# One pool for the normed blocks and the up weights, three early loads of the down part, and a written order for the last tiles of a hybrid decoder layer

## The chip, the cores and the metric

One NeuronCore of a Trainium2 chip runs the whole kernel. The metric is device time in microseconds of one execution. Five engines work side by side, each through its own queue in the order of that queue: TensorE (PE, matmuls; PEld are its weight loads), VectorE (DVE), ScalarE (ACT), GpSimd (POOL) and SyncE (SP), which here issues every DMA.

## The reference

One layer of a hybrid decoder in float32 on 1024 tokens of width 1024. Two mixers (gated DeltaNet and GLA) make `merged`; the change touches what follows. Cut to that:

```python
x = x + rms_norm(merged @ w_o[l], norm_mix_post[l])
h = rms_norm(x, norm_mlp_pre[l])
u = jnp.square(jax.nn.relu(h @ w_mlp_up[l]))          # 1024 -> 4096
x = x + rms_norm(u @ w_mlp_down[l], norm_mlp_post[l]) # 4096 -> 1024
```

## The kernel before

A float32 product is made of three matmuls: every operand is split into a high part (ACT, `CAST`, tiles `wh`, `s[:,0]`) and a low part (DVE, one subtraction, `wl`, `s[:,1]`), and `mm3` (L256) issues high x high, high x low, low x high. So each operand passes ACT and then DVE before PE can use it.

Both products of the channel mixer use a seven-product scheme on 2x2 blocks (Strassen's, in a form with few sums). The stages that matter here, in the order of the program:

1. **Out projection and norms** (L1060 to L1127, pool `op`). `merged @ w_o`, the two norms, and the transposes give four blocks of the normed input, `X11`, `X21`, `X12`, `X22`, 8 KB a partition each, and from them the seven split right-hand operands of the up product: `R11`, `R21`, `R22` in pool `hp2`, `T1` to `T4` in pool `bot` (tag `big`, four buffers).
2. **Early products** (L1129 to L1151). For the first NE = 8 units, products P1 and P2 (which need only `R11` and `R21`) are made ahead, in pairs of units; their results `e` are stored to `d_p` and `d_u[0]` in DRAM and loaded again later by `again` (tiles `p1`, `c11`). Behind them stand the splits of `T3` and `T4` (L1152 to L1156).
3. **Up** (L1194 to L1354, pool `ml`). 16 units n. `prep(n)` (L1200) loads the unit's up weights as two DMAs into one tile `wu` (three buffers) and makes four sums on DVE (`ss`, and one in place). Then the products P6, P5, P7, P3, P4 (for n >= 8 also P1 and P2), 12 matmuls each, accumulate in two PSUM banks: `A` (names `mr`, `mo`) and `C` (name `g`). Between two products that share a bank, a result is read out (`from_A`, L1246; the sums with `C`), and the next product into that bank waits for it. `u_sums` (L1313) makes three more sums and stores seven blocks to DRAM (`d_u`). For n >= 8 `down_sums` (L1226) also loads blocks of the down weights and stores two sums of them to DRAM (`d_t`); it and `u_sums` share the tag `us` with seven buffers.
4. **Down** (L1357 to L1440, pool `dn`). Seven products P1, P2, P6, P5, P7, P4, P3 of eight steps; a step is 24 matmuls on a pair of row blocks. `fetch` (L1175) loads `ru` from `d_u` and `rv` from the down weights or `d_t` (512 KB each, two buffers), and for two products `rx`, and splits them into `s4` (three buffers). One step, the first of P1, is fetched ahead within the last unit of up (L1347 to L1349), into the places of `R11` and `R21`. The scale of the last norm's weight (L1408) is on ACT.
5. **Last tiles** (L1437 to L1440). As each of the four last banks of P3 is done: a sum (DVE), a square with its row sum (ACT, `jk`), a product with the norm weight (DVE), the inverse root (two POOL operations on `sums`), two `scalar_tensor_tensor` on DVE, two stores. The scheduler orders these.

The order in each engine's queue is made by a list scheduler when the kernel is built: by the order of the program, with priorities (`tc.high_priority`), and by when a buffer of a tag comes free. A pool that is opened where a closed one lay takes its bytes, and a tile in it waits for the old tiles that it covers. Before, pool `ml` lies where `op` lay. Each DMA in SP's queue waits in its turn for the tiles it needs, and all behind it wait too.

Of the kernel before, what the change touches and what calls it, by code (L numbers as in the profile page):

```python
# [16 lines left out]
P = 128  # L17
# [115 lines left out]
def kernel(  # L133
# [923 lines left out]
    wdn = wview(w_mlp_down[0], 32)  # L1057


    with tc.tile_pool(name="op", bufs=1, reuse_waits="tile") as op:  # L1060
        X = {n: op.tile([P, 4, 512], F32, name="X" + n) for n in ("11", "21", "12", "22")}
# [9 lines left out]
        for u in range(2):  # L1071
# [19 lines left out]
            for i in range(4):  # L1091
# [6 lines left out]
                xt = op.tile([P, D], F32, tag="xt", name="xt", bufs=2)  # L1098
# [30 lines left out]
        for n in range(0, NE, 2):  # L1129
            pair = range(n, n + 2)  # L1130
            bank = {}
            for p, k0, blk in (("P1", 0, R["11"]), ("P2", 4, R["21"])):
                for m in pair:
# [17 lines left out]
                    SP.dma_start(out=d_p[m] if p == "P1" else d_u[0][:, m, :], in_=e)  # L1151
        T3, T4 = big(), big()  # L1152
# [17 lines left out]
    def load(pool, tag, src):  # L1170
        raw = pool.tile([P, 2, 512], F32, tag=tag, name=tag, bufs=2) if tag else pool
        SP.dma_start(out=raw, in_=src)
        return raw

    def fetch(p, j, pool, place=None):  # L1175
        b, src, *more = LR[p]
        if place:
            s4, (u, v) = place
# [15 lines left out]
    NU = 16  # L1194
    with tc.tile_pool(name="ml", bufs=1, reuse_waits="tile") as ml:
        RT = dict(P1=R["11"], P2=R["21"], P3=R["22"], P4=T4, P5=T1, P6=T2, P7=T3)
        un = {}
        reserve(ml, (("ev", 512, 10), ("us", 512, 7), ("wu", 2 * KT * P, 3)))

        def prep(n):  # L1200
            raw = ml.tile([P, 2 * KT * P], F32, tag="wu", name="wu", bufs=3).rearrange("p (f k c) -> p f k c", f=2, c=P)
            for f in range(2):
                c0 = (n + NU * f) * P
                SP.dma_start(out=raw[:, f], in_=wup[:, :, c0:c0 + P])
# [150 lines left out]
    bot.release()  # L1355


    with tc.tile_pool(name="dn", bufs=1, reuse_waits="tile") as dn:
        def keep(nm):
            return [dn.tile([P, 512], F32, name=f"{nm}{i}") for i in range(4)]  # L1360

        c12, c22 = keep("c12"), keep("c22")
        reserve(dn, (("xt", D, 4),))
# [43 lines left out]
        c11, c21 = keep("c11"), keep("c21")  # L1407
        act(wpost2, wpost2, AF.Copy, scale=D ** 0.5)  # L1408
# [28 lines left out]
        for i in products("P3", Bb, False, True):  # L1437
            tt(c12[i], Bb[i], c12[i], ALU.add)
# [33 lines left out]
```

## Time and profile before

| | us |
|---|---|
| median of 3 runs | 1728.85 |
| range of the runs | 1727.12 to 1730.13 |
| the profiled execution, its own time | 1728.73 |
| the profiled execution, span of the page | 1727.0 |
| PE busy | 1657.5 (96%) |
| DVE busy | 986.5 (57%) |
| ACT busy | 771.7 (45%) |
| POOL busy | 131.6 (8%) |

The span runs from the first to the last instruction; 1.73 us of the time lie around it. A row of the timeline has start, duration, engine, line, operation, the tiles written and read, and in square brackets how long the engine stood idle before it and what released it. SPq rows are DMA issues. A row of a windows table gives busy time and count of each engine in that stretch, the granted clock of PE, the share of the DMA engines' time, and GB/s.

### The profile page before, as it was taken

The numbers are of one execution on the slowest core, as the hardware profiler recorded it, in microseconds if no ns is written. First come the engines' busy times: TensorE is split into PE (matmuls) and PEld (weight loads), VectorE is DVE, ScalarE is ACT, GpSimd is POOL, SyncE is SP. The second block draws the span as 40 slices with busy tenths as digits, with TensorE's granted clock in tenths as the row PEclk, the third lists the DMA queues.
The fourth block names the chain that finished last, engine by engine and source line by source line (L and its number), as shares of the span: only waits on it lengthen the run. The fifth ranks groups of instructions, "written<-read, shape, count | busy, mean of one in ns | idle before, by whom it ended". The sixth has DMA issues, their size and how long they took to land.

```text
span 1727.0 us, 24474 instructions
## 1 busy us (share of the span) xinstructions
PE 1657.5 (96%) x9174; PEld 1401.2 (81%) x9174; DVE 986.5 (57%) x1678; ACT 771.7 (45%) x1577; POOL 131.6 (8%) x221
## 2 busy tenths in 40 slices
PE   7999999999999999999999999889999979999997
PEld 6887778878899998998788877667788858888886
DVE  5677565862544436642445365777777754555664
ACT  5456545643533335433321255634455544443442
POOL 2010111111001000101000021000000000000021
PEclk9999999999999999999999999989999989999999
DMA  5222213322211121124634344566588888577775
GB/s 165 56 77 70 83 41 89 86 68 70 67 49 50 50 62 44 37 62 158 204 108 140 129 161 155 176 227 218 184 276 293 270 273 279 192 237 246 231 253 184
DMA packets 186405, 251.39 MB, mean 146 GB/s; under 512 B 23351, under 2 KB 108430, under 8 KB 186286
## 3 DMA queue, kind: packets, MB, share of 16 engines
q1 hardware_dynamic: 186286, 249.83, 45.0%
q8 instruction: 72, 1.18, 0.3%
q14 instruction: 47, 0.39, 0.1%
HBM read 185.79 MB, written 63.98 MB: 145 GB/s over the span
## 4 chain that ended last, share of the span: by engine, by line
PE 81%; DVE 6%; ACT 5%; DMA 5%; issue 2%; POOL 1%; SPq 0%; DVEq 0%; ACTq 0%; POOLq 0%
PE g L67 55%; PE mr L67 9%; PE mo L67 8%; PE ml L67 3%; PE mt L67 3%; DMA gb<-d_g 2%; PE mt L71 1%; DVE Xt L165 1%; DVE Xi L547 1%; ACT wh L236 1%; ACT E L177 1%; DMA oraw<-d_ob 1%; DVE wl L165 1%; DMA d_sig<-sg 1%; ACT Zp L603 0%
## 5 line engine op out<-in xcount | busy, mean ns | idle before, releaser
L165 DVE TENSOR_TENSOR wl<-w,wh 128x512 fp32r<-128x512 f32 x181 | 125.7, 695 | 229.6 <-ACT wh L236 228.1
L67 PE MATMUL g<-hT,wh 128*128 128x512 f32 (+1 forms) x600 | 239.5, 399 | 1.3 <-DVE gr L174 0.9
L67 PE MATMUL g<-hL,wh 128*128 128x512 f32 (+1 forms) x600 | 233.1, 388 | 0.0
L67 PE MATMUL g<-hT,wl 128*128 128x512 f32 (+1 forms) x600 | 232.3, 388 | 0.0
L236 ACT CAST wh<-w 128x512 fp32r<-128x512 f32 x184 | 114.0, 619 | 212.6 <-PE g L67 189.1
L67 PE MATMUL g<-s 128*128 128x512 f32 x768 | 177.6, 393 | 11.6 <-ACT s L1189 11.6
L67 PE MATMUL g<-wh,hT 128*128 128x256 f32 x640 | 185.1, 289 | 0.0
L67 PE MATMUL g<-wl,hT 128*128 128x256 f32 x640 | 181.5, 284 | 0.0
L67 PE MATMUL g<-wh,hL 128*128 128x256 f32 x640 | 181.4, 284 | 0.0
L67 PEld LDWEIGHTS g<-s 128*128 128x128 f32 x768 | 145.6, 190 | 43.0 <-ACT s L1189 12.0
L165 DVE TENSOR_TENSOR s<-ru,s 128x1024 fp32r<-128x1024 f32 x55 | 67.4, 1225 | 124.6 <-ACT s L1189 124.3
L67 PEld LDWEIGHTS g<-hT,wh 128*128 128x128 f32 x600 | 113.8, 190 | 21.6 <-DVE gr L174 1.1
L67 PEld LDWEIGHTS g<-hT,wl 128*128 128x128 f32 x600 | 113.7, 189 | 21.6 <-DVE wl L165 0.2
L67 PEld LDWEIGHTS g<-hL,wh 128*128 128x128 f32 x600 | 113.9, 190 | 18.7 <-issue 1.0
L1189 ACT CAST s<-ru 128x1024 fp32r<-128x1024 f32 x55 | 57.9, 1053 | 150.9 <-PE g L67 73.0
L67 PEld LDWEIGHTS g<-wh,hT 128*128 128x128 f32 x640 | 122.4, 191 | 1.4 <-issue 1.0
L67 PEld LDWEIGHTS g<-wl,hT 128*128 128x128 f32 x640 | 122.6, 191 | 1.2 <-issue 1.0
L67 PEld LDWEIGHTS g<-wh,hL 128*128 128x128 f32 x640 | 122.5, 191 | 0.1
L177 ACT ACTIVATE c<-c 128x512 f32<-128x512 f32 x104 | 64.8, 631 | 38.8 <-DVE c L165 37.2
L67 PE MATMUL g<-wh,big 128*128 128x512 f32 x256 | 80.4, 392 | 0.0
L67 PE MATMUL mr<-big,wh 128*128 128x512 f32 x192 | 61.7, 403 | 11.1 <-ACT wh L236 11.1
L165 DVE TENSOR_TENSOR s<-rv,s 128x1024 fp32r<-128x1024 f32 x55 | 67.0, 1219 | 3.2 <-ACT s L1189 3.2
(419 smaller groups left out, 3383.7 us busy)
## 6 DMA issues: line engine op xcount, KB each, us to landing
ru<-d_u SPq DMA_DIRECT2D x55, 512.0 KB, 4.3
w<-in_w_in_dram SPq DMA_DIRECT2D x80, 256.0 KB, 2.7
rv<-in_w_mlp_down_dram SPq DMA_DIRECT2D x39, 512.0 KB, 5.4
wu<-in_w_mlp_up_dram SPq DMA_DIRECT2D x32, 512.0 KB, 5.1
d_u<-c SPq DMA_DIRECT2D x56, 256.0 KB, 2.8
d_u<-us SPq DMA_DIRECT2D x48, 256.0 KB, 2.0
us<-in_w_mlp_down_dram SPq DMA_DIRECT2D x48, 256.0 KB, 4.7
xt<-in_x_dram SPq DMA_DIRECT2D x16, 512.0 KB, 5.2
```

Of the source, the lines that this page charges most:

```text
L67: return self.eng.matmul(out, lhsT, rhs, start=start, stop=stop, skip_group_check=more)
L71: return self.eng.transpose(out=out, in_=in_, identity=identity)
L165: (eng or V).tensor_tensor(out=out, in0=a, in1=b, op=op)
L177: A.activation(out=out, in_=a, func=func, **kw)
L236: A.copy(out=hi, in_=raw)
L547: V.tensor_reduce(out=X[:, :, i:i + 1], in_=tv, axis=AX.X, op=ALU.add)
L1189: A.copy(out=s4[:, i], in_=raw)
```

## The change

Four edits, all in stages 1, 3, 4 and 5 above.

**One pool z.** A pool `z` is opened ahead of `op` and lives until the end of up. Its tag `wu` has four buffers: first they hold `X12`, `X11`, `X21`, `X22`, then the up weights. `prep(0)` stands ahead of the splits of `T3` and `T4` in the program. The tag `ss` (two buffers) holds the tiles `xt` of stage 1, then the sums of `prep`. The fourth sum of `prep` is now made in place of `L12`: in `prep` itself for the first eight units, and behind P2 (which needs the old value) for the others, by `fourth`.

**Three early steps of down.** `ahead` holds three steps of P1 in place of one, loaded into the places of `R11` and `R21`. The split tiles of all steps come from the four `big` buffers, which `bot` keeps until the end. The tags `ru`, `rv`, `rx` have three buffers, reserved first so that they lie on the bytes of `z`; the kept results of down lie in the places of `R11` and `R22`. The tag `us` has six buffers in place of seven.

**Norm weight on POOL.** The scale of `wpost2` moves from ACT to POOL.

**Last tiles.** The order on DVE, ACT and POOL is that of the program: `final(i - 1)` behind the sum and square of tile i.

```diff
+    z = tc.alloc_tile_pool(name="z", bufs=1, reuse_waits="tile")
+    reserve(z, (("wu", 2 * KT * P, 4), ("ss", D, 2)))
+    def ztile():
+        return z.tile([P, 2 * KT * P], F32, tag="wu", name="wu", bufs=4)
...
+            tt(L21, L11, L21, ALU.subtract)
+        un[n] = dict(P1=L11, P2=L12, P3=L12, P4=L22, P5=ss[:, 0], P6=ss[:, 1], P7=L21)
+        if n < NE:
+            fourth(n)
+    def fourth(n):
+        with tc.high_priority(offset=HP):
+            tt(un[n]["P3"], un[n]["P3"], un[n]["P6"], ALU.subtract)
...
-        X = {n: op.tile([P, 4, 512], F32, name="X" + n) for n in ("11", "21", "12", "22")}
+        X = {n: ztile().rearrange("p (k c) -> p k c", c=512) for n in ("12", "11", "21", "22")}
...
-                xt = op.tile([P, D], F32, tag="xt", name="xt", bufs=2)
+                xt = z.tile([P, D], F32, tag="ss", name="xt", bufs=2)
...
+        prep(0)
         T3, T4 = big(), big()
...
-        raw = pool.tile([P, 2, 512], F32, tag=tag, name=tag, bufs=2) if tag else pool
+        raw = pool.tile([P, 2, 512], F32, tag=tag, name=tag, bufs=3) if tag else pool
...
-            s4 = pool.tile([P, 4, 2, 512], F32R, tag="s4", name="s4", bufs=3)
+        s4 = big().rearrange("p (q k) c -> p q k c", q=4)
...
-        reserve(ml, (("ev", 512, 10), ("us", 512, 7), ("wu", 2 * KT * P, 3)))
+        reserve(ml, (("ev", 512, 10), ("us", 512, 6)))
...
             product(n, "P2", b, True)
+            fourth(n)
...
-                    ahead = [fetch("P1", 0, None, (s4, (r4[:, 0:2], r4[:, 2:4])))]
+                    r = [hp2.tile([P, 8, 512], F32, tag=t, name="r" + t) for t in ("R11", "R21")]
+                    places = [(r[q // 2][:, q % 2 * 4:q % 2 * 4 + 2], r[q // 2][:, q % 2 * 4 + 2:q % 2 * 4 + 4])
+                              for q in range(3)]
+                    ahead = [fetch("P1", 2 * q, None, places[q]) for q in range(3)]
...
-        act(wpost2, wpost2, AF.Copy, scale=D ** 0.5)
+        ts(wpost2, wpost2, D ** 0.5, ALU.mult, eng=G)
...
-        for i in products("P3", Bb, False, True):
-            tt(c12[i], Bb[i], c12[i], ALU.add)
-            half(c12[i], i, 1)
-            final(i, c11[i], c12[i])
+        with tc.manual_schedule(engines={ET.DVE, ET.Activation, ET.Pool}):
+            for i in todo:
+                tt(c12[i], Bb[i], c12[i], ALU.add)
+                half(c12[i], i, 1)
+                if i:
+                    final(i - 1, c11[i - 1], c12[i - 1])
+            final(3, c11[3], c12[3])
```

Three places show how the queues move. The first is SP's queue at the end of the early products. Before, `e` are the early results, `wu_10947` and `wu_10959` the weights of units 0 and 1, and `p1`, `c11` the loads of `again`:

```order
L1151 DMA d_p_102<-e_10795 128x512
L1151 DMA d_u0_93<-e_10816 128x512
L1151 DMA d_u0_93<-e_10838 128x512
L1151 DMA d_p_102<-e_10861 128x512
L1151 DMA d_p_102<-e_10883 128x512
L1151 DMA d_u0_93<-e_10904 128x512
L1151 DMA d_u0_93<-e_10926 128x512
L1204 DMA wu_10947<-in_w_mlp_up_dram 128x8x128 x2
L1222 DMA p1_10955<-d_p_102 128x512
```

Of the change, the same stretch; `wu_10935`, `wu_10963`, `wu_10994`, `wu_11115` are the weights of units 0 to 3:

```order
L1180 DMA d_p_102<-e_10800 128x512
L1072 DMA wu_10935<-in_w_mlp_up_dram 128x8x128 x2
L1180 DMA d_u0_93<-e_10821 128x512
L1072 DMA wu_10963<-in_w_mlp_up_dram 128x8x128
L1180 DMA d_u0_93<-e_10843 128x512
L1072 DMA wu_10963<-in_w_mlp_up_dram 128x8x128
L1180 DMA d_p_102<-e_10866 128x512
L1072 DMA wu_10994<-in_w_mlp_up_dram 128x8x128
L1180 DMA d_p_102<-e_10888 128x512
L1072 DMA wu_10994<-in_w_mlp_up_dram 128x8x128
L1180 DMA d_u0_93<-e_10909 128x512
```

The weights of unit 0 moved ahead of six stores of early results, and those of units 1 to 3 stand between the stores; the loads of `p1` and `c11` stay behind the last store.

The second place is DVE's queue in unit 0 of up. Before, `wl_10973`, `wl_11000`, `wl_11016`, `wl_11038`, `wl_11057` are the low parts for P6, P5, P7, P3 and P4 of unit 0, and `c12_10988` the sum that reads bank `A` (`mr`) ahead of P7:

```order
L165 TENSOR_TENSOR wl_11016<-wu_10947,wh_11015 128x512
L165 TENSOR_TENSOR ss_10962<-wu_10959 128x512
L165 TENSOR_TENSOR ss_10962<-ss_10962,wu_10959 128x512
L165 TENSOR_TENSOR wu_10959<-wu_10959 128x512
L165 TENSOR_TENSOR ss_10962<-wu_10959,ss_10962 128x512
L165 TENSOR_TENSOR wl_11038<-ss_10950,wh_11037 128x512
L165 TENSOR_TENSOR c12_10988<-mr_10971,p1_10955 128x512
L165 TENSOR_TENSOR ss_10993<-wu_10990 128x512
L165 TENSOR_TENSOR wl_11057<-wu_10947,wh_11056 128x512
```

Of the change, `wl_11020`, `wl_11042`, `wl_11061` are the low parts for P7, P3 and P4, and `c12_10992` that sum:

```order
L165 TENSOR_TENSOR wl_11020<-wu_10935,wh_11019 128x512
L165 TENSOR_TENSOR ss_10997<-wu_10994 128x512
L165 TENSOR_TENSOR ss_10997<-ss_10997,wu_10994 128x512
L165 TENSOR_TENSOR wu_10994<-wu_10994 128x512
L165 TENSOR_TENSOR wu_10994<-wu_10994,ss_10997 128x512
L165 TENSOR_TENSOR wl_11042<-wu_10935,wh_11041 128x512
L165 TENSOR_TENSOR wl_11061<-wu_10935,wh_11060 128x512
L165 TENSOR_TENSOR c12_10992<-mr_10975,p1_10959 128x512
```

The sum `c12` stood between the low parts for P3 and P4; now it stands behind both.

The third place is SP's queue in the last unit of up. Before, `c11_13105`, `c22_13239` are results of unit 15, the `us` with `in_w_mlp_down` are loads of `down_sums`:

```order
L1244 DMA d_u0_93<-c11_13105 128x512
L1244 DMA d_u3_96<-us_13177 128x512
L1244 DMA d_u4_97<-us_13178 128x512
L1244 DMA d_u5_98<-c12_13037 128x512
L1230 DMA us_13245<-in_w_mlp_down_dram 128x512
L1244 DMA d_u6_99<-us_13179 128x512
L1230 DMA us_13247<-in_w_mlp_down_dram 128x512
L1230 DMA us_13249<-in_w_mlp_down_dram 128x512
L1230 DMA us_13302<-in_w_mlp_down_dram 128x512
L1244 DMA d_u2_95<-c22_13239 128x512
```

Of the change; `rR11` and `rR21` are the second and third early step of down:

```order
L1202 DMA rR11_13259<-d_u0_93 128x1024
L1202 DMA rR11_13259<-in_w_mlp_down_dram 128x2x512
L1258 DMA d_u3_96<-us_13181 128x512
L1258 DMA d_u4_97<-us_13182 128x512
L1258 DMA d_u5_98<-c12_13040 128x512
L1202 DMA rR21_13260<-d_u0_93 128x1024
L1202 DMA rR21_13260<-in_w_mlp_down_dram 128x2x512
L1244 DMA us_13249<-in_w_mlp_down_dram 128x512
L1258 DMA d_u6_99<-us_13183 128x512
L1258 DMA d_u2_95<-c22_13243 128x512
L1244 DMA us_13251<-in_w_mlp_down_dram 128x512
L1244 DMA us_13253<-in_w_mlp_down_dram 128x512
```

Four loads of 512 KB came in, and all but one of the last loads of `down_sums` now stand behind the store of `c22` of unit 15.

More of the change, by code (lines that the diff above doesn't have):

```diff
@@ L1177, in fetch @@
         if place:
-            s4, (u, v) = place
+            u, v = place
             load(u, None, d_u[b][:, j:j + 2, :])
@@ L1228, in down_sums @@
             for f, c in ((1, 1), (0, 1), (0, 0)):
-                w.append(ml.tile([P, 512], F32, tag="us", name="us", bufs=7))
+                w.append(ml.tile([P, 512], F32, tag="us", name="us", bufs=6))
                 SP.dma_start(out=w[-1], in_=wdn[:, f * NU + j, c * 512:c * 512 + 512])
@@ L1315, in u_sums @@
             x = un.pop(n)
-            s1, s2, s4 = (ml.tile([P, 512], F32, tag="us", name="us", bufs=7) for _ in range(3))
+            s1, s2, s4 = (ml.tile([P, 512], F32, tag="us", name="us", bufs=6) for _ in range(3))
             tt(s1, x["c12"], x["c22"], ALU.add)
@@ L1324, in u_sums @@
             store(6, n, s4)
-        prep(0)
         again(0)
@@ L1354 @@
             u_sums(n)
-    bot.release()
+    z.release()
     with tc.tile_pool(name="dn", bufs=1, reuse_waits="tile") as dn:
[L1359 to L1363, printed above, removed]
+        reserve(dn, (("ru", 2 * 512, 3), ("rv", 2 * 512, 3), ("rx", 2 * 512, 3)))
         wpost2 = dn.tile([P, D], F32, name="wpost2")
@@ L1369, in products @@
             for j in range(0, NU, 2):
-                todo.append((j, ahead.pop() if ahead else fetch(p, j, dn)))
+                todo.append((j, ahead.pop(0) if ahead else fetch(p, j, dn)))
                 if tail and j == NU - 4:
                     continue
+                if tail and j == NU - 2:
+                    yield None
                 for i in range(4):
@@ L1406 @@
         plain("P1", Ab, True)
-        c11, c21 = keep("c11"), keep("c21")
-        act(wpost2, wpost2, AF.Copy, scale=D ** 0.5)
+        kept = [hp2.tile([P, 8, 512], F32, tag=t, name="c" + t) for t in ("R11", "R22")]
+        c11, c21, c12, c22 = ([kept[q // 2][:, q % 2 * 4 + i] for i in range(4)] for q in range(4))
+        ts(wpost2, wpost2, D ** 0.5, ALU.mult, eng=G)
         sums = dn.tile([P, P], F32, name="sums")[:, 0:3 * NTOK].rearrange("p (t c) -> p t c", c=3)
@@ L1436 @@
             final(4 + i, c21[i], c22[i])
-        for i in products("P3", Bb, False, True):
-            tt(c12[i], Bb[i], c12[i], ALU.add)
-            half(c12[i], i, 1)
-            final(i, c11[i], c12[i])
+        ET = mybir.EngineType
+        todo = products("P3", Bb, False, True)
+        next(todo)
+        with tc.manual_schedule(engines={ET.DVE, ET.Activation, ET.Pool}):
[5 more added lines that the diff above has]
+            final(3, c11[3], c12[3])
     hp2.release()
+    bot.release()
 _INS = ['x', 'w_in', 'conv_w', 'a_log', 'dt_bias', 'gdn_norm', 'gla_gate_w2', 'gla_gate_b', 'gla_norm',
```

29 lines of the change are left out of this document (12 added, 17 removed).

## The prediction

> **What bounds the kernel now.** First the page: PE is busy nearly always, so only stretches in which it stands still can be won.
>
> ```profile
> span 1727.0 us, 24474 instructions
> PE 1657.5 (96%) x9174; PEld 1401.2 (81%) x9174; DVE 986.5 (57%) x1678; ACT 771.7 (45%) x1577; POOL 131.6 (8%) x221
> ```
>
> Then the list of waits of PE. Its two longest single ones are these (11.6 and, within the 11.1, one of 9.6):
>
> ```profile
> PE g L67 <- ACT s L1189: 11.6, 1, 11.6
> PE mr L67 <- ACT wh L236: 11.1, 4, 9.6
> ```
>
> The timeline places them. The first lies between the early products and up: PE ends at 1117.40, the weights of unit 0 are issued at 1119.14, behind the last store of `e`, and DVE has both halves at 1124.90.
>
> ```profile
> 1117.01 0.39 PE L67 MATMUL mo<-R,wl 128*128 128x512 f32 x1
> 1119.14 1.13 SPq L1204 DMA_DIRECT2D wu<-in_w_mlp_up_dram  x2
> 1124.90 0.69 DVE L165 TENSOR_TENSOR ss<-wu 128x512 f32<-128x512 f32 x1 [12.52 <-DMA wu<-in_w_mlp_up_dram]
> 1127.02 1.22 PE L67 MATMUL mr<-big,wh 128*128 128x512 f32 x2 [9.63 <-ACT wh L236]
> 1132.61 0.89 PE L67 MATMUL g<-big,wh 128*128 128x512 f32 x2
> ```
>
> The second lies between up and down: the one early step ends at 1403.07, the next step's second load is issued at 1406.27, and PE starts when ACT has split it.
>
> ```profile
> 1398.37 4.70 PE L67 MATMUL g<-s 128*128 128x512 f32 x20
> 1406.27 0.45 SPq L1172 DMA_DIRECT2D rv<-in_w_mlp_down_dram  x1
> 1413.58 1.04 ACT L1189 CAST s<-rv 128x1024 fp32r<-128x1024 f32 x1
> 1414.67 10.65 PE L67 MATMUL g<-s 128*128 128x512 f32 x34 [11.61 <-ACT s L1189]
> ```
>
> A wait also costs what comes behind it, since the granted clock falls to half in it. The chain of waits gives the full pace, 12 matmuls in 2.72 and 192 in 43.52 (0.2267 each); the windows give the clock (the column before the last two).
>
> ```profile
> 1114.68 2.73 PE mo L67 x12
> 1499.22 43.52 PE g L67 x192
> 1119.00:1120.00 1.00, 0.00 (x0) 0.00 (x0) 0.00 (x0) 0.00 (x0) 0.00 (x0) 0.75 0.48 162
> 1406.00:1407.00 1.00, 0.00 (x0) 0.00 (x0) 0.00 (x0) 0.00 (x0) 0.00 (x0) 0.61 1.26 373
> 1418.00:1420.00 2.00, 2.00 (x7) 1.54 (x6) 0.40 (x1) 1.01 (x1) 0.00 (x0) 0.53 1.27 253
> 1420.00:1422.00 2.00, 2.00 (x11) 1.62 (x10) 1.23 (x1) 0.04 (x1) 0.00 (x0) 1.00 0.72 273
> 1240.00:1402.00 162.00, 162.00 (x715) 133.89 (x714) 114.68 (x179) 89.35 (x152) 0.00 (x0) 1.00 0.79 265
> 1384.00:1392.00 8.00, 8.00 (x37) 6.58 (x36) 7.05 (x10) 5.30 (x8) 0.00 (x0) 1.00 0.35 136
> 1403.07:1414.67 11.60, 0.00 (x0) 0.00 (x0) 2.30 (x4) 3.15 (x3) 0.00 (x0) 0.64 1.03 341
> 1414.67:1708.00 293.33, 293.29 (x1282) 242.29 (x1283) 165.07 (x154) 125.23 (x148) 11.04 (x8) 0.99 0.73 241
> ```
>
> After the first wait P6 of unit 0 took 1127.02 to 1132.61, 5.59 for 2.72: 2.87 lost. After the second, the clock is half until about 1419.9 (0.53 as a mean of 1418 to 1420), so of 5.2 us half is lost: 2.6. The first wait costs 9.63 + 2.87 = 12.5, the second 11.61 + 2.6 = 14.2. In the rest of up and of down PE has no idle time (162.00 of 162.00, 293.29 of 293.33).
>
> **The change, part by part.** *The weights of unit 0 earlier.*
>
> ```profile
> 1102.02 0.32 SPq L1151 DMA_DIRECT2D d_p<-e  x1
> 1102.79 0.69 DVE L165 TENSOR_TENSOR big<-X,big 128x512 fp32r<-128x512 f32 x1
> 1109.83 0.69 DVE L165 TENSOR_TENSOR wl<-w,wh 128x512 fp32r<-128x512 f32 x1
> 1127.40 0.61 ACT L236 CAST wh<-wu 128x512 fp32r<-128x512 f32 x1
> wu<-in_w_mlp_up_dram SPq DMA_DIRECT2D x32, 512.0 KB, 5.1
> p<-d_p SPq DMA_DIRECT2D x8, 256.0 KB, 4.4
> us<-in_w_mlp_down_dram SPq DMA_DIRECT2D x48, 256.0 KB, 4.7
> ```
>
> In SP's new order the weights come behind the store at 1102.02 and wait for the last reading of `X12`, which ends at 1103.48. The second half is issued near 1104.1 and lands 5.1 later, 1109.2. DVE reaches the sums behind the `wl` of 1109.83, at 1110.4; four of them and the splits of P6 take to about 1113.6. PE wants them at 1117.40, so this wait goes whole, with its slow matmuls. SP is held at 1103.48 and again near 1107 for the weights of unit 1 (`X11`); behind it wait stores of `e` that were not ready before 1105.79 and 1109, so nobody notices.
>
> What is late next is P7 of unit 0. It adds into the bank that `c12` reads first, and `c12` now stands in DVE's queue behind the low part for P4, whose `wh` on ACT needs a buffer that P5 frees. P6 and P5 run to 1117.40 + 2 x 2.72 = 1122.84; `wh` takes 0.61, `wl` 0.69, `c12` 0.69: P7 starts near 1124.9, a new wait of 2.1. The load of `p1`, which `c12` also needs, is still behind the last store of `e`: issued near 1120.0, landing 4.4 later, 1124.4, so at worst it adds some 0.3. Bounds of this wait: 2.0 and 3.3 (`p1` 1 us later still). Gain: 12.5 - 2.1 = 10.4.
>
> *Three early steps.* They give PE 67 matmuls behind the end of up (72 less the five that its order has earlier), 67 x 0.2267 = 15.2 in place of 4.5. With up ending 0.4 later (below), the fourth step is wanted at 1398.4 + 0.4 + 15.2 = 1414.0. When is it there?
>
> ```profile
> 1386.93 1.04 ACT L1189 CAST s<-r 128x1024 fp32r<-128x1024 f32 x1
> 1388.39 0.58 ACT L1250 COPY c<-mo 128x512 f32<-128x512 f32 x1
> 1392.75 0.69 DVE L165 TENSOR_TENSOR c<-g,c 128x512 f32<-128x512 f32 x1 [0.51 <-ACT c L1250]
> 1394.80 0.33 SPq L1244 DMA_DIRECT2D d_u<-c  x1
> r<-in_w_mlp_down_dram SPq DMA_DIRECT2D x1, 512.0 KB, 5.6
> ```
>
> The loads of the second and third step are issued from about 1383.6 to 1389.4, where the DMA engines were busy 0.35: room is there. But two queues are in order. On ACT the early splits stand among the copies of unit 15: the first waits for a `big` buffer until P6 is done, so the copy of 1388.39 comes near 1389.0 and P7 0.4 later; the sum of 1392.75 comes behind four low parts, near 1394.0, which P3 waits for. P4 fills most of that, so up ends 0.4 later. Then the split of the third step waits for its load (issued near 1389.0, 5.6 to land: 1394.6) and stands ahead of the two passes that make `c22`. The store of `c22` goes from 1394.80 to about 1397.0, and behind it in SP's queue stand five loads of `down_sums`, the last issued near 1398.9 and landing 4.7 to 5.3 later, 1404. Four more DVE sums (2.1) and the stores follow before SP comes to the loads of the fourth step: the second of them near 1407.5, where the second step's was at 1406.27. That one took 7.3 to its split (1413.58), with the DMA engines full (1.03); with two more stores in flight I take 8.3, then the split of 1.04: 1416.9. So a wait of 2.9 is left, three steps further on. Bounds: 0 (landing as fast as the median 4.7 of `us` allows) and 11.6 (nothing gained). I take 2.9, since the chain is one of rows with small errors. Gain: 14.2 - 2.9 = 11.3.
>
> *The clock in the new waits.* In the first old wait it fell about 2.1 us after the last matmul (0.75 in 1119 to 1120), in the second 3.1 us after (0.61 in 1406 to 1407). So a wait of 2.1 rarely meets a fall and one of 2.9 does about as often as not. I count one fall, 2.6, in the second.
>
> [...]
>
> *Last tiles.*
>
> ```profile
> 1711.71 1.41 DVE L174 SCALAR_TENSOR_TENSOR c<-c,sums,xt 128x512 f32<-128x512 f32 x2 [0.84 <-POOL sums L1396]
> 1713.93 2.88 PE L67 MATMUL mo<-s 128*128 128x512 f32 x12
> 1718.22 0.63 ACT L177 ACTIVATE jk<-c 128x512 f32<-128x512 f32 x1 [3.68 <-DVE c L165]
> 1722.46 1.40 DVE L174 SCALAR_TENSOR_TENSOR c<-c,sums,xt 128x512 f32<-128x512 f32 x2
> ```
>
> DVE no longer waits for POOL, but each tile still takes sum 0.65, square 0.75 on ACT, product 0.65 and a pair of 1.35: 3.4, for PE's 2.72. From the second tile at 1711.4 the fourth starts at 1718.2 and ends, with two pairs, 4.75 later: 1723.0 for 1723.86. Gain 0.9; bounds 0.3 and 1.5.
>
> *At nothing:* `fourth` and the smaller `ss` (as many DVE operations as before), three buffers for `ru`, `rv`, `rx` and four for split tiles (PE waited for none in down), results kept in `R11`, `R22`. The weight's scale on POOL is first used where P2 ends, over 40 us later; if it took 40 it would show. Six `us` buffers: a load waits for one more store; DVE has 162 - 114.68 = 47 us to spare over the eight units, 5.9 each, which covers the 4.7 of a load.
>
> Sum, against the profiled execution's own 1728.73 (1.73 around its span; 0.12 under the median): 1728.73 - 10.4 - 11.3 - 0.9 + 2.6 = **1708.7**.
>
> **The rivals.** *No clock lost in the new waits:* 1706.1. For it, they are short; against, the fall after 2.1. If both lose it, 1711.5.
>
> *Both waits vanish:* the fourth step's loads land before 1413 and `c12` is not held. 12.5 + 14.2 + 0.9 = 27.6: 1701.1. For it, the DMA engines' idle time near 1388; against, the DVE order of unit 0 is fixed.
>
> *The second wait only moves:* DMA engines are full from 1403 on (1.03) and the fourth step comes as late as 11.6 after the third ends: 1728.73 - 10.4 - 0.9 = 1717.4. For it, the bytes are the same; against, 2 MB of them moved to where the share was 0.35.
>
> *The change doesn't do what it says:* the weights wait for the X blocks longer than I read, and both waits stay in large part: 1720 to 1729.
>
> *Slower:* with six `us` buffers the last load of each unit's `down_sums` waits for a store, DVE stands at it in order, and the low parts behind are late for PE, in eight units. At 20.1 / 8 = 2.5 us a unit it eats the gain, at 3.0 the time is 1732.7. For it, the DMA share of 0.79; against, the 5.9 us of spare DVE time a unit.
>
> **How the numbers follow.** Forecast (one clock fall, or two) 0.40; none 0.22; both waits vanish 0.16; the second moves whole 0.12; not as said 0.06; slower 0.04. The range goes from 1700.5 (both vanish, and the tail gives its 1.5) to 1715.5 (two thirds of the wait that only moves); about 0.16 lies outside. A difference of 0.2%, 3.5 us, is what a measurement of this kernel can tell. Faster by more: 0.94, within 0.02 (part of "not as said"), slower 0.04.
>
> **What would show it.** Right: no idle PE at 1117, P6 of unit 0 in 2.72, a wait of about 2 us ahead of its P7 released by `c12`; PE busy for 16 us behind up, then a wait near 3 us for ACT's split of the fourth step; SP's load of it near the same distance from up's end as before. Wrong: a PE wait in units 8 to 15 of up, released by `wl` or `wh`; the fourth step's wait at 0 or above 6; the last pair on DVE more than 2 us earlier against the last matmul.

## The result, and the profile after

| | us |
|---|---|
| before, median of 6 runs | 1728.55 (1727.12 to 1730.13) |
| changed, median of 6 runs | 1718.42 (1716.20 to 1721.56) |
| ratio, 95% interval | 0.9941 (0.9929 to 0.9954) |
| changed, the profiled execution | 1717.46, span 1715.8 |

Faster by 10.1 us. The forecast was 1708.7, 20 us faster, with a range of 1700.5 to 1715.5: half of the gain did not come. Both long waits of PE are gone, as forecast. These are the page of the changed kernel and its list of PE's waits.

```profile
span 1715.8 us, 24483 instructions
PE 1659.6 (97%) x9174; PEld 1402.4 (82%) x9174; DVE 987.4 (58%) x1678; ACT 769.1 (45%) x1576; POOL 135.5 (8%) x222
```

```profile
PE mr L67 <- DVE c L165: 3.3, 1, 3.3
...
PE g L67 <- ACT big L1219: 2.4, 1, 2.4
...
PE mr L67 <- ACT c L1264: 1.1, 1, 1.1
PE mo L67 <- ACT c L1264: 1.0, 1, 1.0
```

11.6 and 9.6 have become 3.3 and 2.4. The last two rows are new: PE waits within up, where it had no idle time behind 1240 before.

**Unit 0 of up** (timeline of the changed kernel, PE, DVE and SP). PE reaches P7 at 1125.69 and stands still until 1128.97. `c12` stands behind the low part for P4 (1126.15) as forecast, but that is not what ends last: it waits 1.29 more for `p1`. The load of `p1` was issued at 1122.74, 2.49 behind the end of the early products (1120.25 in this execution); the forecast had it 2.6 behind (1120.0 and 1117.40), so its place in SP's queue is as forecast. What differs is how long it took: 5.40 from its issue to the start of `c12`, where the forecast took 4.4, the median of the eight loads of `p1`. In the kernel before, this one load of unit 0 already took 5.4 (last line, the DMA issues of the kernel before within 1120 to 1121).

```profile
1119.86 0.39 PE L67 MATMUL mo<-R,wl 128*128 128x512 f32 x1
...
1125.30 0.39 PE L67 MATMUL g<-big,wl 128*128 128x512 f32 x1
...
1128.97 1.05 PE L67 MATMUL mr<-big,wh 128*128 128x512 f32 x2 [3.28 <-DVE c L165]
...
1126.15 0.69 DVE L165 TENSOR_TENSOR wl<-wu,wh 128x512 fp32r<-128x512 f32 x1 [0.20 <-ACT wh L236]
...
1128.14 0.69 DVE L165 TENSOR_TENSOR c<-mr,p 128x512 f32<-128x512 f32 x1 [1.29 <-DMA p<-d_p]
...
1122.74 0.69 SPq L1236 DMA_DIRECT2D p<-d_p  x1
```

```profile
p<-d_p SPq DMA_DIRECT2D x1, 256.0 KB, 5.4
```

**Units 1 to 5.** The same `c12` is late in these units too, by so little that no list of waits shows it: P5's matmuls start 0.23 apart, the last starts at 1159.60, so P7 could start at 1159.83, and it starts at 1160.08, when `c12` (1159.26, behind a low part and two sums) has read the bank. A unit takes 14.76 from one `wh` wait to the next, where it took 14.46.

```profile
1159.60 0.39 PE L67 MATMUL g<-big,wl 128*128 128x512 f32 x1
1160.08 0.70 PE L67 MATMUL mr<-big,wh 128*128 128x512 f32 x2
...
1163.57 0.73 PE L67 MATMUL mo<-big,wh 128*128 128x512 f32 x2 [0.48 <-ACT wh L236]
...
1178.33 0.73 PE L67 MATMUL mr<-big,wh 128*128 128x512 f32 x2 [0.48 <-ACT wh L236]
...
1159.26 0.68 DVE L165 TENSOR_TENSOR c<-mr,p 128x512 f32<-128x512 f32 x1
```

The kernel before, PE:

```profile
1167.88 0.73 PE L67 MATMUL mo<-big,wh 128*128 128x512 f32 x2 [0.48 <-ACT wh L236]
...
1182.34 0.73 PE L67 MATMUL mr<-big,wh 128*128 128x512 f32 x2 [0.48 <-ACT wh L236]
```

**Units 8 to 15.** Cut at the first matmul of P2 of the next unit (24 matmuls on `g`, P2 and then P3), a unit takes 19.04 of pure work. Three of the changed kernel, n = 11 to 13, took 19.40, 20.49 and 20.33: 3.1 us in all. The window of n = 12:

```profile
1317.94:1338.43 20.49, 19.36 (x85) 15.69 (x84) 14.04 (x22) 10.19 (x19) 0.00 (x0) 1.00 0.82 264
```

**The end of up and of the kernel.** The three early steps run from 1398.26 for 15.35; the fourth starts at 1415.99 after 2.38 of idle time, released by ACT's split, and the last matmul ends at 1703.25 + 2.88 = 1706.13. DVE ends at 1709.83 + 2.74 = 1712.57, 6.44 behind it (7.04 before).

```profile
1398.26 15.35 PE L67 MATMUL g<-big 128*128 128x512 f32 x67
...
1415.99 4.30 PE L67 MATMUL g<-big 128*128 128x512 f32 x11 [2.38 <-ACT big L1219]
...
1703.25 2.88 PE L67 MATMUL mo<-big 128*128 128x512 f32 x12
...
1709.83 2.74 DVE L174 SCALAR_TENSOR_TENSOR cR<-cR,sums,xt 128x512 f32<-128x512 f32 x4
```

**The ledger.** The same points of the program in both profiles. The first is the last group of transposes into `mt` ahead of the early products; then a `wh` wait in unit 1, the first cut above in two units, PE's end, and the span's end.

| point | before | after | shift | of this stretch | forecast |
|---|---|---|---|---|---|
| transposes | 1094.46 | 1097.33 | +2.87 | +2.87 | 0 |
| unit 1 | 1139.06 | 1134.03 | -5.03 | -7.90 | -10.4 |
| first cut | 1245.01 | 1241.42 | -3.59 | +1.44 | 0 |
| last cut | 1378.29 | 1377.80 | -0.49 | +3.10 | 0 |
| PE's end | 1716.81 | 1706.13 | -10.68 | -10.19 | -11.3 + 2.6 = -8.7 |
| span | 1727.01 | 1715.75 | -11.26 | -0.58 | -0.9 |

So the forecast missed by 8.8 in this execution: 2.9 in a stage that the change doesn't touch, 2.5 in the first wait, 1.4 and 3.1 in units of up for which it counted nothing; the second wait gave 1.5 more than forecast.

### The profile page after: what moved, and what is told of

Its sections match the earlier page's. It is cut to its first block, busy times and chain, and to the rows that moved or that the text cites. A ratio compares the mean times of both kernels' runs of the same rounds, so it can differ in the third digit from the quotient of the medians.

```text
span 1715.8 us, 24483 instructions
## 1 busy us (share of the span) xinstructions
PE 1659.6 (97%) x9174; PEld 1402.4 (82%) x9174; DVE 987.4 (58%) x1678; ACT 769.1 (45%) x1576; POOL 135.5 (8%) x222
## 5 line engine op out<-in xcount | busy, mean ns | idle before, releaser
L67 PE MATMUL g<-big 128*128 128x512 f32 x768 | 176.7, 392 | 2.4 <-ACT big L1219 2.4
L67 PEld LDWEIGHTS g<-big 128*128 128x128 f32 x768 | 145.2, 189 | 33.1 <-ACT big L1219 2.8
L165 DVE TENSOR_TENSOR big<-ru,big 128x1024 fp32r<-128x1024 f32 x53 | 64.9, 1224 | 115.9 <-ACT big L1219 115.5
L1219 ACT CAST big<-ru 128x1024 fp32r<-128x1024 f32 x53 | 55.8, 1053 | 154.8 <-PE g L67 57.7
L165 DVE TENSOR_TENSOR big<-rv,big 128x1024 fp32r<-128x1024 f32 x53 | 64.5, 1218 | 0.1
```

The source lines that it names most:

```text
L67: return self.eng.matmul(out, lhsT, rhs, start=start, stop=stop, skip_group_check=more)
L165: (eng or V).tensor_tensor(out=out, in0=a, in1=b, op=op)
L1219: A.copy(out=s4[:, i], in_=raw)
```

## The experiments

Each kernel is the changed one with one more edit, unless it says otherwise. The times are medians, against 1718.42 of the changed kernel; the ratios are against runs of the kernel before on the same chip. Single runs of one kernel differ by 1 to 11 us, so the trace is asked each time for the place. A profile is one execution too: the same rows of up lost 3.1 in units 8 to 15 of the changed kernel, 2.9 in e3 and 5.8 in e14.

| | median (runs) | ratio to before, 95% interval |
|---|---|---|
| e9, weights of unit 0 late | 1726.63 (11) | 0.9987 (0.9979 to 0.9996) |
| e4, one early step | 1725.22 (11) | 0.9983 (0.9975 to 0.9992) |
| e14, last tiles as before | 1719.32 (4) | 0.9946 (0.9930 to 0.9961) |
| e3, `prep(0)` moved in the text | 1718.02 (6) | 0.9942 (0.9926 to 0.9957) |
| e2, `c12` first | 1715.52 (6) | 0.9932 (0.9919 to 0.9945) |
| e5, `c12` first and `p1` early | 1710.71 (4) | 0.9894 (0.9881 to 0.9908) |
| e1, seven `us` buffers | 1716.82 (6) | 0.9940 (0.9920 to 0.9960) |
| e8, six down loads together | 1715.68 (5) | 0.9925 (0.9912 to 0.9939) |
| e10, both | 1716.47 (5) | 0.9927 (0.9915 to 0.9939) |
| e13, both and a shorter loop | 1715.12 (5) | 0.9922 (0.9910 to 0.9935) |
| e7, down loads in idle buffers | 1711.37 (4) | 0.9901 (0.9888 to 0.9915) |
| e6, four early steps | 1712.18 (5) | 0.9912 (0.9896 to 0.9927) |
| e11, e5 and e7 | 1704.75 (4) | 0.9861 (0.9848 to 0.9875) |
| e12, e5, e7 and e6 | 1704.08 (4) | 0.9858 (0.9843 to 0.9873) |

**What each part of the change is worth.** e3 puts the request for unit 0's weights back in the text:

```diff
-        prep(0)
         T3, T4 = big(), big()
...
+        prep(0)
         again(0)
         prep(1)
```

> The changed kernel with unit 0's weights asked for where the kernel before asked for them, behind the early products' stores, all else as changed. Theory: PE's idle time ahead of P6 of unit 0 comes back in most of its length (8 to 10 us, and slow matmuls behind it), the 3.28 ahead of P7 goes; the earlier loading is worth 6 to 8 us net: 1725 to 1726. Rival: the shared pool, not the place of the request, decides, and the time stays near 1718.

1718.02. The scheduler made the same rows for every engine, so this is the changed kernel a second time and undoes nothing: the shared pool decides, not the place in the text. It is of use as a repeat: its last transpose is at 1094.75, not 1097.33.

e9 undoes the first part by force:

```diff
+        if after is not None:
+            A.copy(out=raw[:, 0, 0, 0:1], in_=after[:, 0:1])
+            A.copy(out=raw[:, 1, 0, 0:1], in_=after[:, 0:1])
         for f in range(2):
...
-        prep(0)
+        prep(0, e)
```

> The changed kernel with the first part undone by force: unit 0's weights are asked for only when the last of the early products has been read (two copies of 128x1 from it into the weights' tile ahead of the loads). Theory: the early loading is worth what the trace says, 9.63 + 2.87 of the kernel before less the new wait of 3.3 and its clock (1.3 to 1.7), 7 to 8 us; without it PE stands still 8 to 9 us ahead of P6 of unit 0, the wait ahead of P7 goes: 1718.4 + 7 = 1725. Rival: PE's wait comes back but something behind it makes up for it (the second stage is bound by loads anyway): under 1721.

1726.63, 8.2 more, and PE stands still again ahead of P6 of unit 0 (timeline of e9, PE):

```profile
1127.95 1.22 PE L67 MATMUL mr<-big,wh 128*128 128x512 f32 x2 [9.96 <-ACT wh L236]
```

The theory holds in the place: from the transposes to the `wh` wait in unit 1 e9 takes 44.29 (1095.06 to 1139.35), the changed kernel 36.70, so the early weights are worth 7.6 there. The time of e9's profiled execution is the longest of its eleven (1730.56), and its units 8 to 15 lose 9.1. e4 undoes the second part:

```diff
-                    ahead = [fetch("P1", 2 * q, None, places[q]) for q in range(3)]
+                    ahead = [fetch("P1", 2 * q, None, places[q]) for q in range(1)]
```

> The changed kernel with one early step of down in place of three, all else as changed. Theory: PE stands still some 11 to 12 us behind the first step again, and the two further early steps are worth about 10 us: 1728 to 1729. Rival: the second wait only moves (the DMA engines are full there and the fourth step comes as late): 1718 to 1720. That the fourth step's wait was 2.4 us in the changed kernel speaks for the theory.

1725.22, 6.8 more; the wait behind the first step is back (timeline of e4, PE):

```profile
1413.40 6.88 PE L67 MATMUL g<-big 128*128 128x512 f32 x18 [10.87 <-ACT big L1219]
```

The rival, a wait that only moves, falls. The gain is less than the 10 expected in the median; in its profile the stretch from the last cut to PE's end is 9.5 longer than in the changed kernel, and its units 8 to 15 lose 6.8. e14 undoes the last tiles:

```diff
-        with tc.manual_schedule(engines={ET.DVE, ET.Activation, ET.Pool}):
-            for i in todo:
...
-                if i:
-                    final(i - 1, c11[i - 1], c12[i - 1])
-            final(3, c11[3], c12[3])
+        for i in todo:
...
+            final(i, c11[i], c12[i])
```

> The changed kernel with the last four tiles in the scheduler's order again (each tile's two final products right behind its own product, not one tile later). Theory: from PE's last matmul to VectorE's last operation it takes 7.04 again as in the kernel before, where the changed kernel took 6.44: 0.6 us worse, too little for the times to tell (1718 to 1719). Rival: the last tiles' order is worth the 0.9 to 1.5 that I took as its upper bound: 7.4 or more.

1719.32, and in its timeline DVE ends at 1712.89 + 1.40 = 1714.29, PE at 1704.31 + 2.88 = 1707.19, 7.10 apart:

```profile
1704.31 2.88 PE L67 MATMUL mo<-big 128*128 128x512 f32 x12
...
1712.89 1.40 DVE L174 SCALAR_TENSOR_TENSOR cR<-cR,sums,xt 128x512 f32<-128x512 f32 x2
```

The last tiles' order is worth 0.66. The two larger parts give 15.0 in these medians, the whole change 10.1: something takes back about 5.

**The wait in unit 0 and the units behind it.** e2 moves only `c12` on DVE:

```diff
-            with tc.high_priority(offset=HPM):
+            with tc.high_priority(offset=4 * HP if n < NE else HPM):
                 from_A(n, x["c12"])
```

> The changed kernel with c12 ahead of the sums for the next unit in VectorE's queue, in units 0 to 7 (only VectorE's order differs). Theory: P7 of units 1 to 6 waits about 0.3 us for c12 in each unit (14.77 us per unit where the kernel before took 14.46), and this goes: 1.5 to 2 us less, about 1716.7; the wait of 3.28 ahead of P7 in unit 0 stays, since c12 there waits for the load of p1. Rival: the rows that c12 overtakes are as urgent, and units take 14.77 still or more: 1718.4 or above.

1715.52. From `wh` wait to `wh` wait the units take 14.38 (timeline of e2, PE), better than 14.46 before; the wait in unit 0 stays, 3.42.

```profile
1146.14 0.74 PE L67 MATMUL mr<-big,wh 128*128 128x512 f32 x2 [0.48 <-ACT wh L236]
...
1160.52 0.73 PE L67 MATMUL mo<-big,wh 128*128 128x512 f32 x2 [0.48 <-ACT wh L236]
```

e5 adds an early load of unit 0's `p1`, into one of the raw-weight buffers that are idle in up:

```diff
+            if n:
+                x["p1"] = ev("p1")
+            else:
+                x["p1"] = wraw.tile([P, 2, 256], F32, tag="w", name="w").rearrange("p a c -> p (a c)")
+            with tc.high_priority(offset=0 if n else HP):
+                SP.dma_start(out=x["p1"], in_=d_p[n])
```

> The changed kernel with c12 ahead of the next unit's sums on VectorE as in the run before, and with unit 0's p1 loaded into an idle buffer ahead of the early products' last stores. Theory: the wait ahead of P7 of unit 0 (3.14 to 3.53 in the runs so far) was for the load of p1 first and for VectorE's order second; with both gone PE goes from the early products through unit 0 without a pause and without the clock's fall there: 3.3 + 1.7 to 3 of clock less than with c12 alone, 1715.5 - 5 = 1710.5. Rival: the wait only passes to the next thing that is late (the low parts on VectorE, 1 to 2 us): 1713 to 1714.

1710.71, as expected. P7 of unit 0 starts 0.53 after P5's last matmul does (timeline of e5, PE; 0.23 is the pace), and the clock does not fall there: P7's own matmuls start 0.23 apart.

```profile
1121.63 0.39 PE L67 MATMUL g<-big,wl 128*128 128x512 f32 x1
...
1122.16 0.70 PE L67 MATMUL mr<-big,wh 128*128 128x512 f32 x2
...
1122.93 0.62 PE L67 MATMUL mr<-big,wh 128*128 128x512 f32 x2
1123.39 0.39 PE L67 MATMUL mr<-big,wl 128*128 128x512 f32 x1
```

So all but some 0.3 of the new first wait was the late arrival of `p1` and `c12`'s place in DVE's queue. The second alone is measured in e11 and e12 (below): there `p1` is early and `c12` stands behind P4's low part again, and the wait is 1.90, near the 2.1 of the forecast.

**The loss in units 8 to 15.** First the number of buffers alone (`us` 7, `ev` 9 in their three places; the orders on PE, ACT and SP stay):

```diff
-        reserve(ml, (("ev", 512, 10), ("us", 512, 6)))
+        reserve(ml, (("ev", 512, 9), ("us", 512, 7)))
```

> The changed kernel with seven us buffers again (ev gets nine instead of ten, so that it fits). Theory: of the missing gain, 3.1 us went in units 8 and 9 of up, where VectorE stood at the sums of the down weights until their loads landed (six buffers), so that ScalarE's copy of A was late for P7 (waits of 1.13 and 0.99 and smaller ones). Then these two waits go and the time falls by about 3 us, from 1718.4 to 1715.4. Rival: the waits come from the order of the rows on ScalarE (the copy behind a wait for VectorE) and not from the buffers: then the waits stay and the time is 1718.4. Nine ev buffers may cost something; then it is above 1718.4.

1716.82. (The two units are n = 12 and 13; the text counts from the first that is cut.) The loss in these units is 1.8 in place of 3.1 (2.9 in e3). The wait ahead of the fourth step is 3.29 in place of 2.38, but it is 3.14 in e3 too, with the rows of the changed kernel, so this doesn't show that it took the gain back. Neither theory as stated. Next SP's order alone:

```diff
+                dw = [down_load(2 * n - NU + q) for q in range(2)]
-                down_sums(2 * n - NU)
+                down_sums(2 * n - NU, dw[0])
...
-                down_sums(2 * n - NU + 1)
+                down_sums(2 * n - NU + 1, dw[1])
```

> The changed kernel with all six down loads of a unit asked for together, six buffers as changed. On SP the last load then stands ahead of the first sums' stores, as in the kernel before, and not behind them. Theory of the order (SP's order, not the number of buffers, makes the last loads late): units 11 to 14 go back to 19.04 and the time falls by about 3: 1715.5. Theory of the buffers: with six of them the loads still wait for stores of the unit before, and units 11 to 14 lose 2 to 3 us as before: 1718.

1715.68, but not for the reason given: its units lose 2.9, spread over five, so the theory of the order falls, and the time was met by chance. Then both:

> The changed kernel with both: six down loads of a unit asked for together, and seven us buffers (nine of ev). Each alone left units 11 to 14 of up a loss of about 2 to 3 us (of 3.1). Theory that it takes both, as in the kernel before: units 8 to 15 take 19.04 each, up ends 3 us earlier, of which the wait ahead of the fourth step takes 0 to 1.5 back: 1715.5 to 1717. Rival: the loss has a third cause (VectorE's order, in which a new sum stands ahead of the next copy), and 2 us of it stay: 1717 to 1718.

1716.47, and the loss is 2.8: neither nor both is the cause. What is left is a closed loop. Here is one round of it in the kernel before (timeline, DVE and SP): the sum that makes `c12` (1307.77), two passes on ACT, the sums of u and their stores, the down loads behind these in SP's queue (the second at 1313.45), the first down sum that needs it (1318.28), and, behind the other down sums in DVE's queue, the next `c12` (1326.81).

```profile
1307.77 0.69 DVE L165 TENSOR_TENSOR c<-g,c 128x512 f32<-128x512 f32 x1 [0.64 <-PE g L67]
...
1313.45 2.42 SPq L1230 DMA_DIRECT2D us<-in_w_mlp_down_dram  x5
...
1318.28 1.42 DVE L165 TENSOR_TENSOR us<-us 128x512 f32<-128x512 f32 x2 [0.62 <-issue]
...
1326.81 0.69 DVE L165 TENSOR_TENSOR c<-g,c 128x512 f32<-128x512 f32 x1 [1.09 <-PE g L67]
```

It takes 5.68 + 4.83 + 8.53 = 19.04, of which DVE waits 1.09 for PE: the loop itself needs 17.95, PE sets the pace. In the changed kernel (timeline, DVE and SP) nothing in the round waits for PE:

```profile
1327.73 0.68 DVE L165 TENSOR_TENSOR c<-g,c 128x512 f32<-128x512 f32 x1
...
1334.25 1.53 SPq L1244 DMA_DIRECT2D us<-in_w_mlp_down_dram  x3
...
1339.57 1.42 DVE L165 TENSOR_TENSOR us<-us 128x512 f32<-128x512 f32 x2 [1.95 <-DMA us<-in_w_mlp_down_dram]
...
1342.26 0.69 DVE L165 TENSOR_TENSOR us<-us 128x512 f32<-128x512 f32 x1 [0.67 <-DMA us<-in_w_mlp_down_dram]
...
1344.94 0.69 DVE L165 TENSOR_TENSOR us<-us 128x512 f32<-128x512 f32 x1 [0.79 <-DMA us<-in_w_mlp_down_dram]
...
1348.08 0.68 DVE L165 TENSOR_TENSOR c<-g,c 128x512 f32<-128x512 f32 x1
```

6.52 + 5.32 + 8.51 = 20.35, and that is what a unit takes there (20.49, 20.33). Part of it is the two late loads (0.67 and 0.79), which e8 and e10 cure; part is ACT, where the two passes that make `c12` stood together before (1308.50, 1.30 for both) and now have a split and the copy of `A` between them (timeline of the changed kernel, ACT):

```profile
1328.44 0.63 ACT L177 ACTIVATE c<-c 128x512 f32<-128x512 f32 x1 [3.01 <-DVE c L165]
1328.98 0.60 ACT L236 CAST wh<-wu 128x512 fp32r<-128x512 f32 x1
1329.49 0.58 ACT L1264 COPY c<-mr 128x512 f32<-128x512 f32 x1
1329.96 0.63 ACT L177 ACTIVATE c<-c 128x512 f32<-128x512 f32 x1
```

In e10 (timeline, DVE and SP) the round is 6.58 + 5.26 + 7.67 = 19.51, for units of 19.46 to 19.82:

```profile
1307.00 0.69 DVE L165 TENSOR_TENSOR c<-g,c 128x512 f32<-128x512 f32 x1
...
1313.58 1.50 SPq L1244 DMA_DIRECT2D us<-in_w_mlp_down_dram  x3
...
1318.84 0.69 DVE L165 TENSOR_TENSOR us<-us 128x512 f32<-128x512 f32 x1 [3.90 <-DMA us<-in_w_mlp_down_dram]
...
1326.51 0.68 DVE L165 TENSOR_TENSOR c<-g,c 128x512 f32<-128x512 f32 x1
```

e13 is e10 with the copy out of the loop:

```diff
-            relu2(x["c12"], x["c12"])
+            with tc.high_priority(offset=4 * HP):
+                relu2(x["c12"], x["c12"])
```

> The run with six loads together and seven buffers, with the two passes that make c12 ahead of the copy of A on ScalarE (in units 9 to 15). In that run each of units 9 to 14 took 19.46 to 19.82. Theory of the loop: down sums to c12's sum 7.8, from there over the two passes, the sums of u and their stores to the second down load 6.6, landing 5.2, together 19.6, which is what a unit took; in the kernel before the same steps took about 7.4 + 5.7 + 4.8 = 17.9, under PE's 19.04. The copy no longer stands in it: 0.5 us less, 19.1, so the units take 19.04 to 19.1, up ends 2 to 2.8 earlier, and the time is 1714 to 1715 for 1716.5, since the wait ahead of the fourth step takes some back. Rival: PE waits for that copy, which now comes 0.5 later: the units take 19.5 or more, 1716.5 to 1719.

1715.12; every unit takes 19.04 (one of the windows of e13, n = 9), and PE has no idle time in them. The edit does more than its text says: in each unit the scheduler also moved two sums ahead of low parts on DVE and a store ahead of the loads on SP. From `c12`'s sum to the issue of the second down load it now takes 6.13 (1306.81 to 1312.94) where e10 took 6.58, and the round is 19.09. Shortening the round takes the whole loss away, and e7 below, which cuts it, does so too, while e1, e8 and e10, in which units still take up to 20.35, 19.97 and 19.82, keep a loss: the loop is the cause.

```profile
1261.94:1280.98 19.04, 19.04 (x85) 15.77 (x84) 14.13 (x24) 10.39 (x19) 0.00 (x0) 1.00 0.90 295
```

Of the 2.8 only 1.35 arrived in the medians, which at ratios of 0.9927 and 0.9922 hardly differ; in the profile the fourth step waits 4.16, 1.2 more than in e10. e7 cuts the loop instead, and takes the loads away from the end of up:

```diff
-                w.append(ml.tile([P, 512], F32, tag="us", name="us", bufs=6))
+                w.append(wraw.tile([P, 2, 256], F32, tag="w", name="w").rearrange("p a c -> p (a c)"))
```

> The changed kernel with the loads of the down weights for the sums in four buffers of the early weights that are idle in this stage, instead of six shared with the sums of u. SP's order changes: the loads and sums go far ahead, none is left for the last units. Theory: units 11 to 14 of up lose 3.1 us because these loads are late for VectorE; they go back to 19.04 each, and the five loads in SP's queue ahead of the fourth step go too, so that its wait shrinks: 1718.4 - 3.1 - 2 to 4 = 1711.5 to 1713.5. Rival: more of this work in units 8 to 11 makes VectorE late there, and the loss only moves: 1717 to 1719.

1711.37. Units at 19.04, and the fourth step waits 1.10. (In unit 0 the wait for `c12` is longer in e7, 4.59, and unit 1 has one of 1.15.)

**The fourth step.** e6 makes four early steps; the last unit's P4 goes ahead of its P3.

```diff
-                              for q in range(3)]
-                    ahead = [fetch("P1", 2 * q, None, places[q]) for q in range(3)]
-                s_P3(n)
+                              for q in range(4)]
+                    ahead = [fetch("P1", 2 * q, None, places[q]) for q in range(4)]
+                if n < NU - 1:
+                    s_P3(n)
                 s_P4(n)
+                if n == NU - 1:
+                    s_P3(n)
```

> The changed kernel with four early steps of down in place of three (P4 of the last unit goes ahead of its P3, so that a buffer for the fourth split is free). Theory: the wait ahead of the fourth step (2.38 to 4.39 in the runs so far) and the clock's fall in it go, since PE has 5.4 us more of work and the next loads come as before: 3 to 5 us less, 1714. Rival: SP's queue and the DMA engines deliver each later step as much later, and the wait stands ahead of the fifth step: 1718.

1712.18. A wait of 1.39 is left, ahead of the fifth step, without a fall of the clock: the ten matmuls behind it take 2.92 (timeline of e6, PE), where the eleven behind the 2.38 of the changed kernel take 4.30. From the last cut to PE's end its profile takes 326.21, the changed kernel 328.33 and e3 330.90, so by the place the fourth step is worth 2.1 to 4.7; the 6.2 between the medians is more than that.

**All together.** e11 has the edits of e5 and e7, e12 also those of e6.

> The changed kernel with c12 first, p1 in an idle buffer, and the down loads in idle buffers. If the three causes are separate, their gains add: 7.7 and 7.0 from 1718.4, 1703.7. Rival: with PE earlier at the end of up, the wait ahead of the fourth step grows by a part of it: 1706.

> As the run with the three, and with four early steps of down. The wait ahead of the fourth step (1.1 to 2.7 us, with the clock's fall in some runs) should go: 1701 to 1703. If instead the loads of the fifth step come as much later, no change from the three together.

1704.75 and 1704.08: 13.7 of the 14.8 that e5 and e7 give one by one, and faster than both kernels (0.9858 of the time before). The time of e11 lies between the theory (1703.7) and its rival (1706); the trace decides for the theory, since the wait ahead of the fourth step is 0.92, not more than e7's 1.10. e12 missed its 1701 to 1703: its trace has no wait of PE left behind up, but with e5 and e7 in, the fourth early step no longer shows in the time (0.7, less than the runs differ). A wait of 1.90 is left in unit 0, where `c12` stands behind P4's low part on DVE again.

## Why the prediction was wrong

*The first wait goes whole: right.* No idle time ahead of P6 of unit 0, and P6 at the full pace.

*P7 of unit 0 waits 2.1 for `c12`, with no fall of the clock: half right.* The place and the instruction are right; the size is the upper bound, 3.3, and for the reason that the bound gives, `p1` landing 1 us later. The term that was mis-sized is its landing: 4.4, the median of eight loads, for a load that took 5.4 in the kernel before and 5.40 here. The clock fell in it (0.50 for 3.4 us; 1.3 of the 2.5 missing); the rows do not decide that, since in e4, with the same rows in unit 0, the matmuls behind a wait of 3.53 start 0.23 apart, the full pace. e5 shows that little else was in it.

*`c12` behind the low part only in unit 0: wrong.* It stands there in the units behind it too, and I priced it once. 0.3 in each of units 1 to 5 makes 1.4; e2 gives it back.

*"At nothing: six `us` buffers ... 47 us to spare over the eight units, 5.9 each, which covers the 4.7 of a load": this step failed.* It cost 3.1 in the profiled execution. Spare time of an engine, averaged over a unit, covers nothing in a chain that closes on itself: what counts is the length of one round, 20.35 against 19.04 (19.51 with the loads as before), whatever DVE does elsewhere in the unit. And the buffers were only the visible part: e1, e8 and e10 leave 1.8 to 2.9, e13 leaves none, with half a microsecond taken from the round by an order on ACT that I had not costed at all. The rival "slower" named the place, but asked for 2.5 a unit to matter, and the waits that came were released by ACT's copy of `A`, not by `wl` or `wh`.

*The fourth step waits 2.9 and the clock falls once: right in the sum, with some luck.* Two terms were off and cancel: the second load was issued at 1407.96, 9.7 behind the start of the 67 matmuls where the forecast had 8.7, and its split began 6.9 later, at 1414.89, where the forecast took 8.3. It came to 2.38 and one fall; the stretch gave 1.5 more than forecast, 0.9 of it in the cost of the fall (at most 1.7, half of 3.4 us at 0.51; forecast 2.6). In the profiles of the kernels with three early steps and the down loads where they were, the wait lay between 2.38 and 4.39. In e13 it took back part of what a shorter up had gained (1.2). Both of its terms vary: the second load is issued 9.1 to 11.0 behind the end of up and split 6.6 to 8.1 later, and in e2 both are long (10.8 and 7.7), in e5 shorter (9.7 and 7.1); why they vary is open. With the down loads gone from there the load is issued 6.3 behind the end of up, and the wait is 1.10 (e7) and 0.92 (e11).

*Last tiles 0.9: right in kind.* 0.58 in the profiles, 0.66 by e14.

*The stage ahead.* 2.9 of the shortfall in the profiled execution lie in a stage that is the same in both kernels. The profile's record of the clock has falls at 129.0 and 845.8 in the changed kernel (0.50 for 3.4 us each), none there before (1.00); e3, the same program, has a mean clock of 0.997 in its profiled execution, where the changed kernel has 0.994, and reaches the transposes 2.6 earlier. That is a matter of the execution. It doesn't rescue the forecast: e3 then lost 2.6 more between the last cut and the end, and both medians are 1718.

The rival without clock loss fell: the clock fell in both new waits (0.50 and 0.51 in the 3.4 us behind them). That the second wait only moves fell with e4. What I didn't consider is that three small new delays, none over 3.1, can take half of a gain that is right.

## What to carry to other kernels

To cost a load that PE will wait for, take the landing of that very load in the profile, not the median of its group. Before calling a smaller pool free, look for a chain that closes on itself through it (compute, store, buffer, load, compute) and add up one round; compare that with the pace of the bounding engine, not with spare time. When a reordering puts an instruction behind another in one unit, look at whether every unit has it, and add up delays too short for the list of waits by comparing the same points of the two traces. And look at what stands behind a stage before speeding it up: a wait there can swallow part of the gain.

## What the runs showed of the hardware

In these runs the length of a wait does not tell whether the granted clock falls. In e4 the matmuls behind the wait of 3.53 in unit 0 start 0.23 apart, the full pace, and behind a wait of 3.20 later in up a pair of them soon takes 1.05 in place of 0.62 (timeline of e4, PE):

```profile
1126.64 0.70 PE L67 MATMUL mr<-big,wh 128*128 128x512 f32 x2 [3.53 <-DVE c L165]
...
1127.41 0.62 PE L67 MATMUL mr<-big,wh 128*128 128x512 f32 x2
1127.87 0.39 PE L67 MATMUL mr<-big,wl 128*128 128x512 f32 x1
...
1348.57 0.73 PE L67 MATMUL mo<-big,wh 128*128 128x512 f32 x2 [3.20 <-ACT c L1264]
...
1350.08 1.05 PE L67 MATMUL mo<-big,wh 128*128 128x512 f32 x2
```

These windows of the changed kernel are three pairs: 3.4 us ahead of a fall and the 3.4 behind it, at the new wait of unit 0, at the fourth step, and in the untouched stage at 845.8 (the column of PE is the busy time, the third from the right the granted clock).

```profile
1125.70:1129.10 3.40, 0.13 (x1) 0.16 (x2) 1.64 (x3) 0.42 (x1) 0.00 (x0) 1.00 1.02 346
1129.10:1132.50 3.40, 3.40 (x9) 2.63 (x10) 0.00 (x0) 0.00 (x0) 0.00 (x0) 0.50 1.04 316
1412.40:1415.80 3.40, 1.21 (x6) 0.67 (x4) 1.07 (x1) 1.95 (x2) 2.46 (x1) 1.00 0.99 374
1415.80:1419.20 3.40, 3.21 (x8) 2.53 (x9) 3.24 (x4) 2.65 (x4) 0.00 (x0) 0.51 1.05 418
842.40:845.80 3.40, 1.19 (x5) 0.67 (x4) 0.74 (x2) 1.81 (x4) 0.52 (x1) 1.00 0.91 293
845.80:849.20 3.40, 3.40 (x9) 2.66 (x8) 1.94 (x3) 1.63 (x3) 0.73 (x2) 0.50 0.70 234
```

In the three stretches ahead PE was busy 0.04 to 0.36 of the time and the clock still stood at 1.00; in those behind it was 0.50 or 0.51, with PE busy again, and from 849.3, 1132.6 and 1419.3 on it was 1.00 once more. e11 and e12 have the same wait of 1.90 in unit 0, and the clock fell in e12 (PE busy 0.44 of the window ahead),

```profile
1122.60:1126.00 3.40, 1.50 (x8) 1.09 (x7) 1.44 (x3) 0.62 (x1) 0.00 (x0) 1.00 1.01 343
1126.00:1129.40 3.40, 3.12 (x9) 1.92 (x7) 0.26 (x1) 0.62 (x1) 0.00 (x0) 0.50 1.06 311
```

and not in e11 (0.55; its clock reads 0.95 in both windows, and 0.947 as the mean of that execution):

```profile
1121.70:1125.10 3.40, 1.86 (x9) 1.21 (x7) 2.32 (x5) 0.62 (x1) 0.00 (x0) 0.95 0.94 260
1125.10:1128.50 3.40, 3.00 (x12) 2.17 (x12) 0.22 (x1) 0.23 (x1) 0.00 (x0) 0.95 1.04 354
```

So waits of 1.90 (e12), 2.38 and 3.28 (the changed kernel) and 3.20 (e4) were followed by a clock of half or its pace, and waits of 1.90 (e11) and 3.53 (e4) were not; what decides it, these runs do not show. A fall of 3.4 us costs up to 1.7, an estimate from those windows: half of it, if PE works throughout. In the kernel before, where PE stood still for 9.63 and 11.61, the clock was 0.50 for 13.6 us each time (from 1119.5 and from 1406.2), and PE worked in 6.1 and 5.1 of them.
